# Three 256-column products in place of a 512-column one, and new address phases for weights and operands

## The chip, the cores and the metric

The kernel runs on one core of a Trainium2 chip. A core has a matrix engine (TensorE, PE in the profile), a vector engine (VectorE, DVE), a scalar engine (ScalarE, ACT), GpSimd (POOL) and the engine that issues most DMAs (SyncE, SP). The metric is the device time of one execution in microseconds. The kernel before takes 966.16 us, the median of three runs (963.55 to 966.61 us).

All work sits in two on-chip memories of 128 partitions: SBUF, which holds tiles, and PSUM, which holds matmul results in banks of 512 float32 per partition. TensorE reads two SBUF operands for each product: a stationary one (here a 128x128 block of weights, loaded by its own LDWEIGHTS instruction) and a moving one, whose columns are streamed through the array (MATMUL).

## The reference

Two layers of a bidirectional encoder trunk work on a sequence of 256 positions with model width 2048, all in float32. Each layer is, in short:

```python
hn = rmsnorm(h, norm_g[i])
u = hn @ w_in[i]                                    # 2048 x 5632
a_val, a_glu, a_z, q, k, v, b_z = split(u)
ya = swish(layernorm(conv31(a_val * sigmoid(a_glu)))) * silu(a_z)
yb = window_attention(q, k, v, bias, sink[i]) * silu(b_z)
h = h + concat([ya, yb]) @ w_out[i]                 # 2048 x 2048
e = rmsnorm(p[i] @ w_pe[i], pe_g[i])                # 256 x 2048
h = h + e * sigmoid(h @ w_pg[i])                    # 2048 x 2048
```

A last RMSNorm closes the trunk. Nearly all arithmetic is in the three large projections.

## The kernel before, in words

**Layout.** Activations lie transposed: channels on the 128 partitions, the 256 positions along the free dimension. A tensor of 2048 channels is 16 blocks of 128x256; a `big` tile holds such a tensor, or the two images (below) of half of it, in 16384 bytes per partition. There are five slots of that size.

**Split products.** TensorE's faster 32-bit form, float32r, keeps fewer bits. So each operand is split into a high image (rounded to float32r) and a low image (the rest), and one block of a projection is the sum of three products: high weight x high operand, high weight x low operand, low weight x high operand. `mm3` (L398) issues them into one accumulation in PSUM.

**Weights.** They stream from HBM as *halves*: 128x1024 float32, eight 128x128 blocks, in the order of `HALVES`. `split` (L163) makes the two images of a half: ACT writes the high one (L169), DVE the low one (L172). The result lies in one of `NSPL = 5` weight buffers, taken in turn; `SHIFT[i]` is the number of float32 by which the images are moved inside buffer i. With `SHIFT = (0, 2, 4, 8, 16)` they start 0, 8, 16, 32 and 64 bytes into the buffer. A weight tile has 2064 float32, which are 8256 bytes or 129 times 64. The operand tiles are all 16384 bytes apart, and high and low image within a tile 8192 bytes.

**Use of a half.** `steps` (L424) takes the next half or halves, and for each of its eight blocks (four in the value projection) calls `mm3`; then `pump` lets the side work (convolution taps, attention, norms) issue some instructions. There is one such call per half. In the first tile of the gate projection two halves are used in turn, block by block (`FIRST_TILES = [(0, 1), ...]`); elsewhere one half follows the other. In the value projection (L626) the roles are changed: the operand is stationary, and the weights move.

**Narrow and wide.** `mm3` has two forms. Narrow (L405 to L407): three MATMULs of 256 columns and three LDWEIGHTS per block, 24 of each per half. Wide (L402, L403), where the PSUM tile has three dimensions: the high weight is loaded once and meets both operand images in one MATMUL of 512 columns, which puts its two results side by side into one bank; the low weight then meets the high image in a MATMUL of 256 columns. That is 16 MATMULs and 16 LDWEIGHTS per half. The wide form is used in the second half of the output projection (`o<-ya`, L782) and in nearly all of the last projection (`g<-h`, `wide` L445, called in L834, L839 and L851). Its two sums have to be added afterwards: in the output projection by two DVE adds per block (L784), in the last one by `merge` (L409), which has a copy on ACT and an add on DVE, ahead of `gate` (L800).

**Order.** PE, DVE and ACT run their instructions in the order in which the code issues them. POOL's are placed by the framework.

Of the kernel before, what the change touches and what calls it, by code (L numbers as in the profile page):

```python
# [10 lines left out]
F32 = mybir.dt.float32  # L11
F32R = mybir.dt.float32r
# [5 lines left out]
P = 128  # L18
D = 2048
S = 256  # L20
DEPTH = 2
KT = D // P
# [16 lines left out]
HALF = 1024  # L39
# [9 lines left out]

NB_FIRST = KT  # L50
NSPL = 5
SHIFT = (0, 2, 4, 8, 16)
MAN = 'DVE,PE,Activation'
LY = (2, 1)
ORD = 1
# [74 lines left out]
def trunk_kernel(ctx: ExitStack, tc: tile.TileContext, xT, pT, wst, par, gain, relb, sinkp, onehot, out):  # L130
    nc = tc.nc
# [3 lines left out]
    big = ctx.enter_context(tc.tile_pool(name="big", bufs=5))  # L135
    wraw = ctx.enter_context(tc.tile_pool(name="wraw", bufs=3))
    wspl = ctx.enter_context(tc.tile_pool(name="wspl", bufs=1))
    cst = ctx.enter_context(tc.tile_pool(name="cst", bufs=1))
    wk = ctx.enter_context(tc.tile_pool(name="wk", bufs=2))
# [2 lines left out]

    def bigt(name, dt=F32):

        return big.tile([P, 2, 8, S], dt, tag="big", name=name)

    def halves(t):
        return [t[:, 0], t[:, 1]]

    def bank(name):  # L150
        return ps.tile([P, 2, S], F32, tag="ps", name=name)
# [11 lines left out]
    def split(h):  # L163
        raw = raws[h // 2][:, h % 2, :]
        i = h % NSPL
        w = wspl.tile([P, 2 * HALF + 16], F32R, tag=f"w{i}", name=f"w{h}")
        w = w[:, SHIFT[i]:SHIFT[i] + 2 * HALF].rearrange("p (t n) -> p t n", t=2)
        hi, lo = w[:, 0], w[:, 1]
        nc.scalar.copy(hi, raw)  # L169
        spl[h] = w  # L170
        if h not in (4, 5):
            nc.vector.tensor_sub(lo, raw, hi.bitcast(F32))  # L172
# [107 lines left out]
    h = halves(bigt("x"))  # L280
# [117 lines left out]
    def mm3(o, w, x, start, stop):  # L398


        if len(o.shape) == 3:
            nc.tensor.matmul(o, w[:, 0], x, start=start, stop=False, skip_group_check=True)  # L402
            nc.tensor.matmul(o[:, 1], w[:, 1], x[:, 0], start=False, stop=stop, skip_group_check=True)  # L403
            return
        nc.tensor.matmul(o, w[:, 0], x[:, 0], start=start, stop=False, skip_group_check=True)  # L405
        nc.tensor.matmul(o, w[:, 0], x[:, 1], start=False, stop=False, skip_group_check=True)  # L406
        nc.tensor.matmul(o, w[:, 1], x[:, 0], start=False, stop=stop, skip_group_check=True)  # L407

    def merge(bs):  # L409

        t = wk.tile([P, 2, S], F32, name="hl", tag="ptt")[:, 0:len(bs), :]
        for x, b in enumerate(bs):
            nc.scalar.copy(t[:, x, :], b[:, 1, :])
            nc.vector.tensor_add(t[:, x, :], b[:, 0, :], t[:, x, :])
        return t

    class Cursor:
        h = 0

    def step(o, X, start, stop):  # L420

        steps([o], X, [start], stop)
# [15 lines left out]
    def pair(X, name):  # L438
        b = bank(name)
        for x in range(2):  # L440
            step(b[:, x, :], X, x == 0, False)
            step(b[:, x, :], X, False, True)
        return b

    def wide(X, name):  # L445

        b = bank(name)
        step(b, X, True, False)
        step(b, X, False, True)
        return b  # L450

    def hilo(hi, lo, src):

        nc.scalar.copy(hi, src)
# [3 lines left out]
    for l in range(DEPTH):  # L458
# [4 lines left out]
        hg = []  # L463
        rbs, subs = [], []

        def operand(k, l=l, h=h, hg=hg):

            i, kk = k // 8, k % 8
            if kk == 0:
                hg.append(bigt(f"hg{l}_{i}", F32R))  # L470
            rb = rbs[0]
            s = wk.tile([P, 2, S], F32, name="hn", tag="u", bufs=3)
            for x in range(2):
                nc.vector.scalar_tensor_tensor(s[:, x, :], h[i][:, kk + x, :], gcol(l, k + x), rb,
                                               ALU.mult, ALU.mult)
            hi, lo = (x[:, kk:kk + 2, :] for x in halves(hg[i]))
            nc.scalar.copy(hi, s)
            return lambda: nc.vector.tensor_sub(lo, s, hi.bitcast(F32))
# [8 lines left out]
        for q in range(4):  # L487
            n = Cursor.h
            Cursor.h += 1
            if l:  # L490
                w = get(n).rearrange("p t (j k c) -> p t j k c", j=4, k=2)
            else:
                raw = raws[n // 2][:, n % 2, :].rearrange("p (j k c) -> p j k c", j=4, k=2)
            for jj in range(0, 4, 2):
                j = 4 * q + jj
                b = bank("e")
                for x in range(2):
                    for k in range(2):
                        if l:
                            mm3(b[:, x, :], w[:, :, jj + x, k, :], pp[:, :, k, :], x == 0 and k == 0, k == 1)  # L500
                        else:
                            nc.tensor.matmul(b[:, x, :], raw[:, jj + x, k, :], pf[:, k, :], start=x == 0 and k == 0,
                                             stop=k == 1, skip_group_check=True)
# [89 lines left out]
        for ts in FIRST_TILES:  # L593
            bs = [bank(f"ag{l}_{t}") for t in ts]
# [14 lines left out]
        b = pair(hg, f"k{l}")  # L609
# [9 lines left out]
        for q in range(4):  # L619
            n = Cursor.h  # L620
            Cursor.h += 1
            w = get(n).rearrange("p t (k c) -> p t k c", k=4)
            for kk in range(4):
                k = 4 * q + kk
# [65 lines left out]
        for i in range(0, 8, 2):  # L690

            b = pair(hg, f"zb{l}_{i}")
            nc.scalar.activation(zb[:, i:i + 2, :], b, AF.Silu)
            b = pair(hg, f"q{l}_{i}")

            qq = wk.tile([P, 2, 2, S], F32R, name="qq", tag="qq")
            for hh in range(2):
                r, o = rows_of[hh], rows_of[1 - hh]
# [7 lines left out]
        for t in range(0, NCT, 2):  # L706
            b = pair(hg, f"za{l}_{t}")
            if t == NCT - 2:
                finish(l)

                for k in (0, 4):
                    nc.gpsimd.dma_start(a[:, k:k + 4, :], hsrc[:, k:k + 4, :])
                yb = bigt(f"yb{l}", F32R)
                nc.scalar.copy(yb[:, 0, 0:2, :], zb[:, 0:2, :])
            nc.scalar.activation(za[:, t:t + 2, :], b, AF.Silu)

        ya = bigt(f"ya{l}", F32R)

        def lnorm(l=l, acc=acc, za=za, ya=ya, ysum=ysum, done=done):

# [42 lines left out]
        Y = [ya, yb]  # L763
        for k in (0, 4):
            nc.gpsimd.dma_start(zb[:, k:k + 4, :], hsrc[:, 8 + k:12 + k, :])
        h1 = []
# [8 lines left out]
        for j in range(0, KT, 2):  # L775
            d = az[:, j // 8, j % 8:j % 8 + 2, :]
            if j % 8 == 0:
                h1.append(bigt(f"h1{l}_{j // 8}", F32R))
            hi, lo = (x[:, j % 8:j % 8 + 2, :] for x in halves(h1[-1]))
            for x in range(2):  # L780
                b = bank(f"o{l}_{j + x}")
                step(b, Y, True, True)  # L782
                for y in range(2):
                    nc.vector.tensor_add(d[:, x, :], b[:, y, :], d[:, x, :])  # L784
            nc.scalar.copy(hi, d)
            sub = lambda d=d, hi=hi, lo=lo: nc.vector.tensor_sub(lo, d, hi.bitcast(F32))
            if j < KT - 2:
                later(sub)
            else:
                sub()  # L790
# [3 lines left out]
        last = l == DEPTH - 1  # L794
# [36 lines left out]
        hparts = []  # L831
        for j in range(0, KT - 2, 2):
            if j:
                bs = [wide(h1, f"g{l}_{j + x}") for x in range(2)]  # L834
            else:
                bs = [bank(f"g{l}_{x}") for x in range(2)]
                for n in range(2):
                    for b in bs:
                        step(b, h1, n == 0, n == 1)  # L839
            gate(j, merge(bs))  # L840
            if j == 4 and not last:
                pp = wk.tile([P, 2, 2, S], F32R, name="pp", tag="qq")
                hilo(pp[:, 0], pp[:, 1], pf)
        for j in range(KT - 2, KT):
            if last and j == KT - 1:
                b = bank(f"g{l}_{j}")[:, 0:1, :]
                step(b[:, 0, :], h1, True, False)
                step(b[:, 0, :], h1, False, True)
                gate(j, b)
            else:  # L850
                gate(j, merge([wide(h1, f"g{l}_{j}")]))  # L851
        drain()
        h = e

# [92 lines left out]
```

## Time and profile before

| | |
|---|---|
| median of three runs | 966.16 us |
| profiled execution | 963.42 us |
| its span, first to last instruction | 961.7 us |
| granted TensorE clock, mean | 0.997 |
| busy: PE, PEld, DVE, ACT, POOL | 948.5, 897.8, 792.2, 558.6, 83.6 us |

The profile was taken of one execution, which lies near the fastest of the three runs. "PE" stands for MATMUL, "PEld" for LDWEIGHTS. In groups and time lines, `g<-h,w` reads: writes tile g, reads tiles h and w; the shapes after it are those of the operands, in partitions x elements, and a MATMUL's second number is its columns. The duration of a MATMUL row (0.28 us for 256 columns) contains its passage through the array; products overlap, and the rate at which PE works is seen in the distance between the starts of two rows, not in their durations.

### The profile page before, as it was taken

What the parts mean: (1) busy time and instruction counts of PE and PEld (TensorE: products, weight loads), DVE (VectorE), ACT (ScalarE), POOL (GpSimd) and SP (SyncE); (2) the same over time, 40 slices, a digit from 0 to 9 for tenths busy, and PEclk for the clock granted to TensorE, in tenths of its full rate; (3) what the DMA queues carried; (4) which work ended last, traced back from release to release, by engine and by line L of the source; (5) the groups of instructions that cost most, each with busy time, mean ns of one, the idle gap of its engine ahead of it and who ended that gap; (6) DMA issues with size and microseconds to landing.
All of it is one profiled execution on the core that took longest, in us unless ns stands there. A gap on an engine that the chain in (4) does not pass through costs nothing.

```text
span 961.7 us, 17740 instructions
## 1 busy us (share of the span) xinstructions
PE 948.5 (99%) x7216; PEld 897.8 (93%) x7216; DVE 792.2 (82%) x1369; ACT 558.6 (58%) x861; POOL 83.6 (9%) x79
## 2 busy tenths in 40 slices
PE   8999999999999999999999999999999999999996
PEld 7999999999999998888899999999999999888885
DVE  3899989998787687887789998998887878677763
ACT  4655455777875553555566444568778545446552
POOL 0022101010000000011103200000100000000111
PEclk9999999999999999999999999999999999999998
DMA  7674546555446464546546455466454555545532
GB/s 292 224 247 175 188 164 238 197 184 188 164 160 242 153 217 165 210 175 230 204 180 220 172 198 201 176 213 206 151 172 169 190 190 193 194 168 183 178 129 88
DMA packets 29005, 182.45 MB, mean 190 GB/s; under 512 B 3595, under 2 KB 4156, under 8 KB 9084
## 3 DMA queue, kind: packets, MB, share of 16 engines
q1 hardware_dynamic: 24284, 165.70, 49.1%
q0 software_dynamic: 3344, 12.88, 4.2%
q10 hardware_dynamic: 1296, 2.75, 0.8%
q8 instruction: 56, 0.92, 0.4%
q14 instruction: 25, 0.20, 0.1%
HBM read 177.09 MB, written 4.23 MB: 189 GB/s over the span
## 4 chain that ended last, share of the span: by engine, by line
PE 94%; DVE 3%; ACT 1%; DMA 1%; issue 0%; POOL 0%; ACTq 0%; DVEq 0%
PE g L402 12%; PE o L402 6%; PE g L403 6%; PE ag L405 6%; PE ag L407 6%; PE ag L406 6%; PE za L405 3%; PE zb L405 3%; PE q L405 3%; PE o L403 3%; PE za L407 3%; PE za L406 3%; PE zb L406 3%; PE q L407 3%; PE zb L407 3%; PE q L406 3%
## 5 line engine op out<-in xcount | busy, mean ns | idle before, releaser
L172 DVE TENSOR_TENSOR w<-raw,w 128x1024 fp32r<-128x1024 f32 x306 | 373.7, 1231 | 96.0 <-ACT w L169 93.4
L169 ACT CAST w<-raw 128x1024 fp32r<-128x1024 f32 x308 | 314.1, 1048 | 142.2 <-PE ag L407 43.0
L580 DVE SCALAR_TENSOR_TENSOR cz<-az,pars,cz 128x241 f32<-128x241 f32 (+11 forms) x480 | 216.8, 501 | 1.0
L402 PE MATMUL g<-h,w 128*128 128x512 f32 x496 | 174.4, 396 | 0.0
L407 PE MATMUL ag<-hg,w 128*128 128x256 f32 x512 | 142.9, 279 | 0.5 <-DVE w L172 0.5
L405 PE MATMUL ag<-hg,w 128*128 128x256 f32 x512 | 143.3, 280 | 0.0
L406 PE MATMUL ag<-hg,w 128*128 128x256 f32 x512 | 142.7, 279 | 0.0
L403 PE MATMUL g<-h,w 128*128 128x256 f32 x496 | 139.0, 280 | 0.0
L402 PEld LDWEIGHTS g<-h,w 128*128 128x128 f32 x496 | 93.1, 188 | 22.6
L407 PEld LDWEIGHTS ag<-hg,w 128*128 128x128 f32 x512 | 96.2, 188 | 0.9 <-DVE w L172 0.9
L405 PEld LDWEIGHTS ag<-hg,w 128*128 128x128 f32 x512 | 96.2, 188 | 0.9 <-ACT w L169 0.8
L406 PEld LDWEIGHTS ag<-hg,w 128*128 128x128 f32 x512 | 96.3, 188 | 0.1
L403 PEld LDWEIGHTS g<-h,w 128*128 128x128 f32 x496 | 93.3, 188 | 0.0
L402 PE MATMUL o<-ya,w 128*128 128x512 f32 x256 | 90.1, 396 | 0.0
L405 PE MATMUL za<-hg,w 128*128 128x256 f32 x256 | 72.9, 285 | 0.0
L405 PE MATMUL q<-hg,w 128*128 128x256 f32 x256 | 72.4, 283 | 0.0
L405 PE MATMUL zb<-hg,w 128*128 128x256 f32 x256 | 72.2, 282 | 0.0
L405 PE MATMUL o<-yb,w 128*128 128x256 f32 x256 | 72.1, 282 | 0.0
L403 PE MATMUL o<-ya,w 128*128 128x256 f32 x256 | 71.7, 280 | 0.0
L407 PE MATMUL za<-hg,w 128*128 128x256 f32 x256 | 71.5, 279 | 0.0
L406 PE MATMUL za<-hg,w 128*128 128x256 f32 x256 | 71.5, 279 | 0.0
L406 PE MATMUL o<-yb,w 128*128 128x256 f32 x256 | 71.5, 279 | 0.0
(224 smaller groups left out, 2076.4 us busy)
## 6 DMA issues: line engine op xcount, KB each, us to landing
raw<-in_wst SPq DMA_DIRECT2D x153, 1024.0 KB, 4.9
bias<-fscr POOLq DMA_DIRECT2D x16, 384.0 KB, 3.8
raw<-in_wst SPq DMA_DIRECT2D x4, 512.0 KB, 8.0
az<-in_xT POOLq DMA_DIRECT2D x4, 512.0 KB, 6.1
hscr<-e POOLq DMA_DIRECT2D x2, 1024.0 KB, 5.1
az<-hscr POOLq DMA_DIRECT2D x4, 512.0 KB, 6.1
x<-in_xT SPq DMA_DIRECT2D x3, 512.0 KB, 8.3
out_t<-og ACTq DMA_DIRECT2D x4, 256.0 KB, 3.2
```

What stands on the lines that cost most here:

```text
L169: nc.scalar.copy(hi, raw)
L172: nc.vector.tensor_sub(lo, raw, hi.bitcast(F32))
L402: nc.tensor.matmul(o, w[:, 0], x, start=start, stop=False, skip_group_check=True)
L403: nc.tensor.matmul(o[:, 1], w[:, 1], x[:, 0], start=False, stop=stop, skip_group_check=True)
L405: nc.tensor.matmul(o, w[:, 0], x[:, 0], start=start, stop=False, skip_group_check=True)
L406: nc.tensor.matmul(o, w[:, 0], x[:, 1], start=False, stop=False, skip_group_check=True)
L407: nc.tensor.matmul(o, w[:, 1], x[:, 0], start=False, stop=stop, skip_group_check=True)
L580: nc.vector.scalar_tensor_tensor(acc[:, t, lo_:hi_], a[:, t, lo_ + s:hi_ + s], w(k), acc[:, t, lo_:hi_], ALU.mult, ALU.add)
```

## The change: narrow products everywhere, other phases

1. `mm3` loses its wide form, and `wide` and `merge` go. The 94 wide halves (32 of the output projection, 62 of the last one) are issued as narrow ones: 24 MATMULs of 256 columns and 24 LDWEIGHTS per half, where there were 16 and 16. Pairs of output blocks share one PSUM bank; one DVE add of 512 columns per pair takes the place of four of 256 in the output projection, and `gate` reads the bank itself.
2. The weight buffers' shifts become 16, 24, 32, 48 and 56 float32 (64, 96, 128, 192 and 224 bytes). A weight tile now has 2112 float32, 8448 bytes or 132 times 64.
3. Operand tiles get phases of their own (`bigx`). A slot of `big` has 24 float32 more, so 16480 bytes, 32 more than a multiple of 64. The tile of the first eight blocks starts at its slot's start, that of the second eight 16 bytes on (`XSHIFT`), and the low image of each lies 8192 + 32 bytes behind the high one (`XLOW`).

```diff
-SHIFT = (0, 2, 4, 8, 16)
+SHIFT = (16, 24, 32, 48, 56)
+XSHIFT = (0, 4)
+XLOW = 8
...
     def bigt(name, dt=F32):
 
-        return big.tile([P, 2, 8, S], dt, tag="big", name=name)
+        return big.tile([P, 16 * S + 24], dt, tag="big", name=name)[:, 0:16 * S].rearrange(
+            "p (t k s) -> p t k s", t=2, k=8)
+
+    def bigx(name, i):
+
+        n = 8 * S + XLOW
+        t = big.tile([P, 16 * S + 24], F32R, tag="big", name=name)[:, XSHIFT[i]:XSHIFT[i] + 2 * n]
+        return t.rearrange("p (t n) -> p t n", t=2)[:, :, 0:8 * S].rearrange("p t (k s) -> p t k s", k=8)
...
-        w = wspl.tile([P, 2 * HALF + 16], F32R, tag=f"w{i}", name=f"w{h}")
+        w = wspl.tile([P, 2 * HALF + 64], F32R, tag=f"w{i}", name=f"w{h}")
...
     def mm3(o, w, x, start, stop):
 
 
-        if len(o.shape) == 3:
-            nc.tensor.matmul(o, w[:, 0], x, start=start, stop=False, skip_group_check=True)
-            nc.tensor.matmul(o[:, 1], w[:, 1], x[:, 0], start=False, stop=stop, skip_group_check=True)
-            return
         nc.tensor.matmul(o, w[:, 0], x[:, 0], start=start, stop=False, skip_group_check=True)
         nc.tensor.matmul(o, w[:, 0], x[:, 1], start=False, stop=False, skip_group_check=True)
         nc.tensor.matmul(o, w[:, 1], x[:, 0], start=False, stop=stop, skip_group_check=True)
...
-                hg.append(bigt(f"hg{l}_{i}", F32R))
+                hg.append(bigx(f"hg{l}_{i}", i))
...
-                yb = bigt(f"yb{l}", F32R)
+                yb = bigx(f"yb{l}", 1)
...
-        ya = bigt(f"ya{l}", F32R)
+        ya = bigx(f"ya{l}", 0)
...
-                h1.append(bigt(f"h1{l}_{j // 8}", F32R))
+                h1.append(bigx(f"h1{l}_{j // 8}", j // 8))
             hi, lo = (x[:, j % 8:j % 8 + 2, :] for x in halves(h1[-1]))
+            b = bank(f"o{l}_{j}")
             for x in range(2):
-                b = bank(f"o{l}_{j + x}")
-                step(b, Y, True, True)
-                for y in range(2):
-                    nc.vector.tensor_add(d[:, x, :], b[:, y, :], d[:, x, :])
+                step(b[:, x, :], Y, x == 0, True)
+            nc.vector.tensor_add(d, b, d)
...
             if j:
-                bs = [wide(h1, f"g{l}_{j + x}") for x in range(2)]
+                b = pair(h1, f"g{l}_{j}")
             else:
-                bs = [bank(f"g{l}_{x}") for x in range(2)]
+                b = bank(f"g{l}_{j}")
                 for n in range(2):
-                    for b in bs:
-                        step(b, h1, n == 0, n == 1)
-            gate(j, merge(bs))
+                    for x in range(2):
+                        step(b[:, x, :], h1, n == 0 and x == 0, n == 1)
+            gate(j, b)
...
         for j in range(KT - 2, KT):
-            if last and j == KT - 1:
-                b = bank(f"g{l}_{j}")[:, 0:1, :]
-                step(b[:, 0, :], h1, True, False)
-                step(b[:, 0, :], h1, False, True)
-                gate(j, b)
-            else:
-                gate(j, merge([wide(h1, f"g{l}_{j}")]))
+            b = bank(f"g{l}_{j}")[:, 0:1, :]
+            for n in range(2):
+                step(b[:, 0, :], h1, n == 0, n == 1)
+            gate(j, b)
```

More of the change, by code (lines that the diff above doesn't have):

```diff
@@ L407, in mm3 @@
         nc.tensor.matmul(o, w[:, 1], x[:, 0], start=False, stop=stop, skip_group_check=True)
[L409 to L415, printed above, removed]
     class Cursor:
@@ L443, in pair @@
         return b
[L445 to L450, printed above, removed]
     def hilo(hi, lo, src):
```

## The prediction, made before the changed kernel was run

> **What bounds the kernel now.** I read the page of the profile first: how busy each engine is, the granted clock, and the chain that ended last.
>
> ```profile
> PE 948.5 (99%) x7216; PEld 897.8 (93%) x7216; DVE 792.2 (82%) x1369; ACT 558.6 (58%) x861; POOL 83.6 (9%) x79
> ...
> PEclk9999999999999999999999999999999999999998
> ...
> PE 94%; DVE 3%; ACT 1%; DMA 1%; issue 0%; POOL 0%; ACTq 0%; DVEq 0%
> ```
>
> PE works nearly all the time at full clock, and the chain runs along it for 94% of the span. Then the list of PE's waits, all of those after the start-up:
>
> ```profile
> PE ag L407 <- DVE w L172: 0.5, 1, 0.5
> PE rfc L355 <- ACT sq L815: 0.4, 1, 0.4
> PE rv0b L369 <- POOL rv0col L362: 0.2, 1, 0.2
> ```
>
> That is 1.1 us. So the time is set by the distance between PE's products, and the groups and the time lines have to say what that is. The groups count them:
>
> ```profile
> L169 ACT CAST w<-raw 128x1024 fp32r<-128x1024 f32 x308 | 314.1, 1048 | 142.2 <-PE ag L407 43.0 <-PE za L407 20.0 <-PE q L407 19.8
> L402 PE MATMUL g<-h,w 128*128 128x512 f32 x496 | 174.4, 396 | 0.0
> L402 PE MATMUL o<-ya,w 128*128 128x512 f32 x256 | 90.1, 396 | 0.0
> ```
>
> 308 halves are split. 496 + 256 = 752 wide MATMULs, eight per half, make 94 wide halves; the other 214 are narrow, 214 x 24 = 5136 products. ACT waits for PE to free weight buffers: PE is what the others wait for.
>
> **What a wide half costs.** Its stages begin and end in these time lines (start in us, duration):
>
> ```profile
> 345.75 0.39 PE L402 MATMUL o<-ya,w 128*128 128x512 f32 x1
> 480.74 0.28 PE L405 MATMUL e<-pp,w 128*128 128x256 f32 x1
> 812.74 0.39 PE L402 MATMUL o<-ya,w 128*128 128x512 f32 x1
> 942.10 0.28 PE L405 MATMUL g<-h,w 128*128 128x256 f32 x1
> ```
>
> In layer 0, 134.99 us hold 16 + 32 = 48 wide halves, in layer 1, 129.36 us hold 46: 2.812 us per half both times. Over the 24 products that the change makes of it, this is 117.2 ns each.
>
> **What a narrow half costs.** The first products of halves 29, 31, 32, 33 and 34 (counted in the order of use; half h lies in buffer h mod 5):
>
> ```profile
> 96.63 0.28 PE L405 MATMUL ag<-hg,w 128*128 128x256 f32 x1
> 102.08 0.28 PE L405 MATMUL ag<-hg,w 128*128 128x256 f32 x1
> 104.91 0.28 PE L405 MATMUL ag<-hg,w 128*128 128x256 f32 x1
> 107.71 0.28 PE L405 MATMUL ag<-hg,w 128*128 128x256 f32 x1
> 110.56 0.28 PE L405 MATMUL ag<-hg,w 128*128 128x256 f32 x1
> ```
>
> Buffers 4 and 0 together: 5.45 us for 48 products, 113.5 ns each. Buffer 1: 2.83/24 = 117.9. Buffer 2: 116.7. Buffer 3: 118.8. Same instruction, same operand tiles; only the weights' address differs. All tile sizes before are multiples of 64 bytes, so the distance from operand to weights, modulo 64, is the shift: 0 in buffers 4 and 0 (64 and 0 bytes), then 8, 16 and 32. So distance 0 is fast, the others cost 3 to 5 ns more. (Buffers 4 and 0 are alike modulo far more than 64, so a longer period isn't excluded.) Longer stretches, with 24, 32 and 10 halves:
>
> ```profile
> 54.83 0.28 PE L405 MATMUL ag<-hg,w 128*128 128x256 f32 x1
> 121.64 0.50 PE L355 MATMUL re0c<-ones,fold 128*128 128x1 f32 x4
> 504.72 0.28 PE L405 MATMUL ag<-hg,w 128*128 128x256 f32 x1
> 594.61 0.28 PE L405 MATMUL v<-w,hg 128*128 128x256 f32 x1
> 605.88 0.28 PE L405 MATMUL zb<-hg,w 128*128 128x256 f32 x1
> 634.14 0.28 PE L648 MATMUL sc<-keys0h,qq 128*128 128x256 f32 x1
> ```
>
> 66.81/576 = 116.0, 89.89/768 = 117.0, 28.26/240 = 117.8 ns. In the third, the same buffers at the same distances no longer reach 113.5: the fast pace is a rhythm that can be missed. For narrow products as a whole I take the first two together, 156.7/1344 = 116.6 ns.
>
> **The change part by part.** *Width.* 94 halves become narrow: 94 x 24 = 2256 products at the new pace r, in place of 117.2 ns. So 752 MATMULs and 752 LDWEIGHTS more cost nothing by themselves: 512 columns already took about two narrow distances. The term is 2256 x (r - 117.2).
>
> *Phases.* All other products change pace too: 5136 x (r - 116.6). One ns of r is worth 7.4 us; this is the whole case. After the change a weight tile is 132 x 64 bytes and an operand slot 32 more than a multiple of 64; with the shifts, weights stand at 0 or 32 modulo 64. The first operand tile's images stand at 0 and 32, the second's at 16 and 48. So in each half on the first tile one image is at distance 0 and the other at 32, on the second tile at 16 and 48; a quarter of the work falls to each. Distance 48 is in no narrow row with the present roles. Its nearest rows are in the value projection, where the weights move (halves 41, 42, and the start of 43):
>
> ```profile
> 131.03 0.28 PE L405 MATMUL v<-w,hg 128*128 128x256 f32 x1
> 133.91 0.28 PE L405 MATMUL v<-w,hg 128*128 128x256 f32 x1
> 136.77 0.28 PE L405 MATMUL v<-w,hg 128*128 128x256 f32 x1
> ```
>
> Half 41 (buffer 1) takes 120.0 ns per product, half 42 (buffer 2, with roles changed at -16, that is 48) 119.2. Bounds for distance 48: 113.5 to 120.0. I take the middle of 116.7 (distance 16) and 119.2, which is 118. The plain mean of the four is then (113.5 + 116.7 + 118.8 + 118)/4, about 116.7.
>
> But the plain mean supposes that a product keeps its pace beside one of another distance. Rows on that are in the first tile of the gate projection, where two halves alternate block by block (halves 8/9, 160/161, 162/163 and 166/167; 504.72 stands above):
>
> ```profile
> 36.77 0.28 PE L405 MATMUL ag<-hg,w 128*128 128x256 f32 x1
> 42.37 0.28 PE L405 MATMUL ag<-hg,w 128*128 128x256 f32 x1
> ...
> 493.37 0.28 PE L405 MATMUL ag<-hg,w 128*128 128x256 f32 x1
> 499.05 0.28 PE L405 MATMUL ag<-hg,w 128*128 128x256 f32 x1
> 510.17 0.28 PE L405 MATMUL ag<-hg,w 128*128 128x256 f32 x1
> 515.82 0.28 PE L405 MATMUL ag<-hg,w 128*128 128x256 f32 x1
> ```
>
> Buffers 3 and 4 alternating, distances 32 and 0: 5.60/48 = 116.7, where the mean of their own paces is 116.2. Buffers 0 and 1 (0 and 8): 118.3 against 115.7. Buffers 2 and 3: 118.1 against 117.7. Buffers 1 and 2: 117.7 against 117.3. Only 4 and 0, both at distance 0, keep 113.5 (504.72 to 510.17). So mixing costs 0.4 to 2.6 ns. The dear case, 0 with 8, doesn't occur after the change; but these rows change distance once in three products, and the change does so twice in every three (high, low, high image). I add 0.7 ns, a little over the 0.5 of 0 with 32: **r = 117.4**. Bounds: 115.6 (no cost of mixing, 48 as fast as 0) and 120.0.
>
> *The adds.* These go or shrink:
>
> ```profile
> L413 ACT COPY hl<-g 128x256 f32<-128x256 f32 x31 | 11.5, 370 | 19.1 <-PE g L403 19.1
> L414 DVE TENSOR_TENSOR hl<-g,hl 128x256 f32<-128x256 f32 x31 | 12.2, 418 | 5.6 <-ACT hl L413 5.6
> L784 DVE TENSOR_TENSOR az<-o,az 128x256 f32<-128x256 f32 x64 | 27.0, 422 | 2.0 <-PE o L403 0.9
> L772 DVE TENSOR_TENSOR az<-o,az 128x512 f32<-128x512 f32 x16 | 11.0, 686 | 1.1 <-PE o L407 1.1
> ...
> 345.75:480.74 134.99, 134.99 (x771) 117.50 (x770) 104.08 (x148) 67.62 (x89) 8.39 (x7) 1.00 0.57 202
> ```
>
> ACT loses 11.5 us, DVE 12.2 + 27.0 - 16 x 0.686 = 28 us. The last row is the stage 345.75 to 480.74 (busy PE, PEld, DVE, ACT): PE fills all 134.99 us while DVE has 31 us to spare, so this is off the path: 0. The only place where a merge could stand on it is the end of layer 0, 0.370 + 0.418 = 0.8 us, and there the next layer's four halves of `w_pe` cover it; in layer 1 the last block has no merge already. Bounds: -0.8 to 0. Operand tiles, weight images and DMAs at other offsets I put at 0 too: no row shows DVE's or ACT's speed hanging on the weights' phase, and DVE and ACT wait for PE, not PE for them. PSUM needs fewer banks.
>
> *Sum.* 5136 x 0.8 ns + 2256 x 0.2 ns = 4.1 + 0.5 = **+4.6 us**, which makes 968.0 of the profiled execution's 963.4 us. The median of the runs, 966.16, is 2.7 us above that execution; the same step is carried over: **970.8 us**, 0.5% slower.
>
> **Rivals.** *Plain mean.* Each product keeps the pace of its own distance, r = 116.7: +0.5 - 1.1 = -0.6 us, 965.5. For it: the first long stretch, 116.0, is the mean of its buffers' own paces. Against it: the alternating halves.
>
> *Faster: the fast rhythm spreads.* Mechanism: distance 0 is fast because the two streams fall into step, and 48 does as well; no operand is left at an odd 8 bytes; no cost of mixing. r = 115.6: -5.1 - 3.6 = -8.7 us, 957.5. It decides from r = 116.4 down, where the two terms come to -2.9 us. Against it: 119.2 in half 42, and that wide halves in buffers 4 and 0 aren't faster than the rest.
>
> *Every product as in half 41.* r = 120.0: 17.5 + 6.3 = +23.8 us, 990. For it: a moving operand not at a multiple of 64, as there. Against it: that offset was 8 bytes, inside a 16-byte unit, and here all are multiples of 16.
>
> *The phases do nothing.* New narrow products run at today's mean: 2256 x (116.6 - 117.2) = -1.4 us, 964.8. The five halves above speak against it. The Trainium skill, page "SBUF — State Buffer", section "Who interferes with whom", would have it so: TensorE has two independent read ports, one for the moving operand and one for LDWEIGHTS, and never waits on anyone. The trace disagrees: with nothing but the weights' address changed, 113.5 becomes 118.8 ns.
>
> **How the numbers follow.** Forecast 0.50; plain mean and phases without effect together 0.28; the rhythm spreads 0.17; as half 41 0.05. A measurement of this kernel tells about 0.3% (2.9 us) from no change. The forecast's lower edge reaches into that, so faster 0.18, same 0.32, slower 0.50. The range goes from the fast rival, 957, to a mixing cost of 2 ns, r = 118.7, +14.2 us: 981 rounded up. The forecast's own range, r = 117.0 to 118.2, is 968 to 977.
>
> **What would show it.** PE's waits stay near 1 us, and no row of L402 with 512 columns is left. 24 products per half in the last projection start 117 to 118 ns apart; halves on the first operand tile and on the second differ, and no stretch of 48 holds 113.5. Wrong it is if such stretches are common, if starts come 116.5 ns apart or 119 and more, or if PE waits for weights.

## The result, and the profile after

The changed kernel takes 972.81 us, the median of three runs (972.66 to 975.30), against 966.16 us before. The comparison of the two gives a ratio of 1.0092, with a 95% interval of 1.0073 to 1.0110: the change makes the kernel 0.9% slower. The profiled execution after takes 972.81 us with a span of 971.0 us; before it was 963.42 us and 961.7 us. So between the two profiles, from which all stages below are read, there are 9.4 us. The medians of before and after are only 6.7 us apart, since the three runs of before lie 0.1 to 3.2 us above its profiled execution.

The page of the changed kernel, in the order in which the prediction read it (busy time of the engines, granted clock, shares of the chain that ended last):

```profile
PE 958.1 (99%) x7968; PEld 941.5 (97%) x7968; DVE 769.8 (79%) x1290; ACT 550.3 (57%) x830; POOL 83.6 (9%) x79
...
PEclk9999999999999999999999999999999999999998
...
PE 94%; DVE 3%; ACT 1%; DMA 1%; issue 0%; POOL 0%; ACTq 0%; DVEq 0%
```

There are 752 MATMULs and 752 LDWEIGHTS more, as worked out, and PE is still the chain, at the same clock. PE is busy for 9.6 us more, and that is the whole loss. From the changed kernel's list of PE's waits (total, times, longest, in us), the longest of the start-up and the longest after it, both as long before:

```profile
PE rh0c L364 <- DVE fold L388: 1.7, 1, 1.7
...
PE ag L412 <- DVE w L181: 0.5, 1, 0.5
```

No wait has been added: the engine starts its products farther apart. Two rows of its groups (busy us, mean ns of one, idle time before it and its cause):

```profile
L410 PE MATMUL g<-h,w 128*128 128x256 f32 x512 | 143.7, 281 | 0.0
L773 DVE TENSOR_TENSOR az<-o,az 128x512 f32<-128x512 f32 x16 | 11.1, 691 | 6.5 <-PE o L412 6.5
```

The last projection has no row with 512 columns left, and DVE waits for PE at its new, wider adds. Where the time went is in the time lines of the changed kernel (start and duration in us) at the same places as before: the beginning and the end of layer 0's former wide stage, then the beginning of layer 1's and the 46th half after it.

```profile
349.07 0.28 PE L410 MATMUL o<-ya,w 128*128 128x256 f32 x1
484.98 0.28 PE L410 MATMUL e<-pp,w 128*128 128x256 f32 x1
820.80 0.28 PE L410 MATMUL o<-ya,w 128*128 128x256 f32 x1
951.45 0.28 PE L410 MATMUL g<-h,w 128*128 128x256 f32 x1
```

In layer 0, 135.91 us hold 48 halves of 24 products: 118.0 ns each, where a wide half came to 117.2. In layer 1, 130.65 us hold 46 halves: 118.3 ns. The stages that were narrow already lose more. From the first gate product (24.08 us before, 23.94 after) to the first row there were 321.7 us before and are 325.1 now; from the second row to the third there were 332.0 and are 335.8. So +3.5 and +3.8 us stand there, and +0.9 and +1.3 in the two stages that were wide: 9.5 us in all.

The same halves as in the prediction, 29 to 34, here the starts of halves 29, 32, 33 and 34:

```profile
97.14 0.28 PE L410 MATMUL ag<-hg,w 128*128 128x256 f32 x1
105.67 0.28 PE L410 MATMUL ag<-hg,w 128*128 128x256 f32 x1
108.52 0.28 PE L410 MATMUL ag<-hg,w 128*128 128x256 f32 x1
111.36 0.28 PE L410 MATMUL ag<-hg,w 128*128 128x256 f32 x1
```

Halves 29 to 31 take 8.53 us, 118.5 ns per product; half 32 takes 118.8, half 33 118.3. The spread between buffers, 113.5 to 118.8 ns before, is nearly gone, and it closed at the slow end. Over all products of the changed kernel whose distance to the next isn't widened by a wait or by other work (at most 126 ns), the mean is 118.05 ns. That is the r of the prediction, which had 117.4.

### The profile page after: what moved, and what is told of

Read it like the earlier page. It is cut to its first block, busy times and chain, and to the rows that moved or that the text cites. A ratio compares the mean times of both kernels' runs of the same rounds, so it can differ in the third digit from the quotient of the medians.

```text
span 971.0 us, 19136 instructions
## 1 busy us (share of the span) xinstructions
PE 958.1 (99%) x7968; PEld 941.5 (97%) x7968; DVE 769.8 (79%) x1290; ACT 550.3 (57%) x830; POOL 83.6 (9%) x79
## 4 chain that ended last, share of the span: by engine, by line
PE 94%; DVE 3%; ACT 1%; DMA 1%; issue 0%; POOL 0%; ACTq 0%; DVEq 0%
PE g L411 6%; PE g L410 6%; PE g L412 6%; PE ag L411 6%; PE ag L410 6%; PE ag L412 6%; PE o L411 6%; PE o L410 6%; PE o L412 6%; PE za L410 3%; PE zb L410 3%; PE q L410 3%; PE q L411 3%; PE za L411 3%; PE zb L411 3%; PE zb L412 3%
## 5 line engine op out<-in xcount | busy, mean ns | idle before, releaser
L181 DVE TENSOR_TENSOR w<-raw,w 128x1024 fp32r<-128x1024 f32 x306 | 374.1, 1231 | 117.2 <-ACT w L178 116.7
L411 PE MATMUL g<-h,w 128*128 128x256 f32 x512 | 143.8, 281 | 0.0
L410 PE MATMUL g<-h,w 128*128 128x256 f32 x512 | 143.7, 281 | 0.0
L412 PE MATMUL g<-h,w 128*128 128x256 f32 x512 | 143.5, 280 | 0.0
L410 PEld LDWEIGHTS g<-h,w 128*128 128x128 f32 x512 | 96.7, 189 | 0.0
L411 PEld LDWEIGHTS g<-h,w 128*128 128x128 f32 x512 | 96.5, 188 | 0.0
L412 PEld LDWEIGHTS g<-h,w 128*128 128x128 f32 x512 | 96.4, 188 | 0.0
L410 PE MATMUL za<-hg,w 128*128 128x256 f32 x256 | 73.2, 286 | 0.0
L410 PE MATMUL q<-hg,w 128*128 128x256 f32 x256 | 72.7, 284 | 0.0
L410 PE MATMUL o<-yb,w 128*128 128x256 f32 x256 | 72.5, 283 | 0.0
L411 PE MATMUL za<-hg,w 128*128 128x256 f32 x256 | 72.0, 281 | 0.0
L411 PE MATMUL q<-hg,w 128*128 128x256 f32 x256 | 72.0, 281 | 0.0
```

## The experiments

Unless a diff says otherwise, each is an edit of the changed kernel. Paces are start to start, per product of 256 columns; "the mean of the clean ones" is the mean over distances of at most 126 ns, as just now. "Distance" is, as in the prediction, the address of the weights less that of the moving operand.

### Width alone, phases alone

The first kernel is narrow everywhere and has the tile sizes and shifts of before:

```diff
-SHIFT = (16, 24, 32, 48, 56)
-XSHIFT = (0, 4)
-XLOW = 8
+SHIFT = (0, 2, 4, 8, 16)
+XSHIFT = (0, 0)
+XLOW = 0
...
-        t = big.tile([P, 16 * S + 24], F32R, tag="big", name=name)[:, XSHIFT[i]:XSHIFT[i] + 2 * n]
+        t = big.tile([P, 16 * S + 0], F32R, tag="big", name=name)[:, XSHIFT[i]:XSHIFT[i] + 2 * n]
-        w = wspl.tile([P, 2 * HALF + 64], F32R, tag=f"w{i}", name=f"w{h}")
+        w = wspl.tile([P, 2 * HALF + 16], F32R, tag=f"w{i}", name=f"w{h}")
```

> The width alone: all products narrow, weights and operands where they were before. Theory (the phases cost, the width does not): the 94 halves that were wide run at the present narrow pace, 116.0 to 117.0 ns per product, so 2256 x (116.5 - 117.2) = -1.6 us, about 964.6 us, not told from no change. Rival (the width costs: 752 more LDWEIGHTS and MATMULs): most of the 6.65 us is here, about 972 us, and the products of the last projection start 119 ns apart or more.

Measured: 961.96 us against 964.37 us of before on the same chip, ratio 0.9971 (0.9958 to 0.9984). Four starts of this kernel, at the places used above:

```profile
347.16 0.28 PE L410 MATMUL o<-ya,w 128*128 128x256 f32 x1
480.79 0.29 PE L410 MATMUL e<-pp,w 128*128 128x256 f32 x1
812.64 0.28 PE L410 MATMUL o<-ya,w 128*128 128x256 f32 x1
940.71 0.28 PE L410 MATMUL g<-h,w 128*128 128x256 f32 x1
```

The 48 halves of layer 0 take 133.63 us, 116.0 ns per product, where the wide form took 134.99 us; the 46 of layer 1 take 128.07 us, 116.0 ns. So with the old phases the narrow form gains 1.4 and 1.3 us, and the two stages that were narrow before stay at 321.7 and 331.9 us. 752 more instructions of each kind cost nothing, as the prediction put it.

The second has the new tile sizes and shifts and keeps the two forms of `mm3`, with `wide`, `merge` and what calls them as before:

```diff
     def mm3(o, w, x, start, stop):
+        if len(o.shape) == 3:
+            nc.tensor.matmul(o, w[:, 0], x, start=start, stop=False, skip_group_check=True)
+            nc.tensor.matmul(o[:, 1], w[:, 1], x[:, 0], start=False, stop=stop, skip_group_check=True)
+            return
...
```

> The phases alone: the wide products stay, weights and operands lie as in the changed kernel. Theory: the 5136 narrow products go from 116.6 to 118.0 ns, +7.2 us, and the wide ones stay near 2.81 us per half, so about 973 us. Rival (the width costs): near 966 us.

Measured: 970.91 us against 964.37, ratio 1.0067 (1.0052 to 1.0082). The stages that are narrow in it take 325.2 and 335.8 us, as in the changed kernel; the wide ones take 134.88 us for the 48 halves of layer 0 and 129.40 us for the 46 of layer 1, where it was 134.99 and 129.36 before. Its group of wide products in the last projection:

```profile
L411 PE MATMUL g<-h,w 128*128 128x512 f32 x496 | 174.2, 396 | 0.0
```

Before, the same row had 396 ns as well. So the loss comes from the phases, and over a whole stage only narrow products feel them. (Single wide halves differ a little from buffer to buffer: before, those of layer 0 took 2.793 us in buffer 1 and 2.826 us in buffers 0 and 3.) The new phases cost 6.5 us on 5136 narrow products, 10.9 us on 7392 (972.81 less 961.96); in its own stages the width is a gain of 1.4 and 1.3 us with the old phases and a loss of 0.9 and 1.3 us against before with the new ones.

### Which distances are fast

The prediction took distances modulo 64 and called 0 the fast one. Two kernels test this. In the first every weight image stands at distance 0 from every operand image, modulo 256 too; in the second at distance 64.

Both put the operand tiles back to 16384 bytes apart with no shift of their own; in the first a weight tile has 8192 bytes.

```diff
-SHIFT = (16, 24, 32, 48, 56)
-XSHIFT = (0, 4)
-XLOW = 8
+SHIFT = (0, 0, 0, 0, 0)
+XSHIFT = (0, 0)
+XLOW = 0
...
-        w = wspl.tile([P, 2 * HALF + 64], F32R, tag=f"w{i}", name=f"w{h}")
+        w = wspl.tile([P, 2 * HALF + 0], F32R, tag=f"w{i}", name=f"w{h}")
```

> The changed kernel with no shift at all: every weight buffer and every operand image begins at the same address modulo 8192 bytes (modulo 64 too). Theory (distance 0 modulo 64 is fast, and stays fast where nothing else is mixed in): all products at 113.5 ns, 7392 x (113.5 - 118.05) = -33.6 us against the changed kernel, about 940 us. Rival (the period is longer than 64 bytes and only a distance of 64 is fast): about 118 ns, 972 us or more. Second rival (the fast rhythm comes from the change between buffers): slower than before, about 970 us.

Measured: 987.94 us against 964.37, ratio 1.0239 (1.0224 to 1.0255). Starts of halves 136 and 156 in this kernel:

```profile
434.99 0.28 PE L410 MATMUL g<-h,w 128*128 128x256 f32 x1
492.59 0.28 PE L410 MATMUL e<-pp,w 128*128 128x256 f32 x1
```

57.60 us for 480 products: 120.0 ns, and each half took 2.880 us. The distance that the prediction took for the fast one is slower than every half with the usual roles in its rows (113.5 to 118.8 ns), and it has the "120.0" of its dearest rival.

For distance 64, with the changed kernel's weight tiles:

```diff
-SHIFT = (16, 24, 32, 48, 56)
+SHIFT = (16, 16, 16, 16, 16)
+XSHIFT = (0, 0)
+XLOW = 0
```

> As the kernel without shifts, but all weight buffers 64 bytes on (all at distance 64 modulo 256 from the operands, as buffers 4 and 0 before). Theory (period of 64 bytes): the same time as without shifts, about 940 us. Rival (only the distance of 64 is fast, period 128 or more): this one 940 us and the one without shifts 972 us.

Measured: 954.54 us, ratio 0.9889 (0.9866 to 0.9912). Starts of halves 100, 122, 262 and 310:

```profile
321.99 0.28 PE L410 MATMUL o<-yb,w 128*128 128x256 f32 x1
384.18 0.28 PE L410 MATMUL o<-ya,w 128*128 128x256 f32 x1
804.35 0.28 PE L410 MATMUL o<-yb,w 128*128 128x256 f32 x1
934.91 0.28 PE L410 MATMUL g<-h,w 128*128 128x256 f32 x1
```

Between the first two, 62.19/528 = 117.8 ns; between the last two, 130.56/1152 = 113.3 ns. The instructions and the distance are the same in both stretches. So 64 bytes is not the period (0 and 64 would be alike), distance 64 can run at 113.3 ns, and it has a second, slower rhythm, which it kept in layer 0 from half 99 to half 155 once it had fallen into it.

### A table of distances

The changed kernel with one shift per half in place of one per buffer: in the output projection's second half and the last projection, six halves each at distances 0, 16, 32 and so on, up to 112 in layer 0 and from 128 to 240 in layer 1. Four stretches of six halves near the start of each layer have other distances, and the rest is at 64. Here and in the kernels below, but for the one on mixing, the operand tiles lie 16384 bytes apart again.

```diff
+SHIFT = (0, 0, 0, 0, 0)
+XSHIFT = (0, 0)
+XLOW = 0
+def shift_of(h):
+    l, r = divmod(h, NHALF)
+    if r >= 108:
+        return 4 * ((r - 108) // 6 + 8 * l)
+    if 14 <= r < 38:
+        return ((2, 18, 34, 50), (16, 48, 32, 24))[l][(r - 14) // 6]
+    return 16
...
-        w = w[:, SHIFT[i]:SHIFT[i] + 2 * HALF].rearrange("p (t n) -> p t n", t=2)
+        w = w[:, shift_of(h):shift_of(h) + 2 * HALF].rearrange("p (t n) -> p t n", t=2)
```

> A scan of distances in one kernel. All operand images at one phase; the weights' distance to them (modulo 256 bytes) is 64 except here: the last 48 halves of layer 0 take 0, 16, ... 112 bytes, six halves each, those of layer 1 128 to 240, and four stretches of six halves at the start of each layer take 8, 72, 136, 200 and 64, 192, 128, 96. Theory (a distance sets the pace, with a period over 64 bytes): the paces repeat what is known, 0 at 120.0, 8 near 118, 32 near 118.8, 64 at 113.3 or 117.8, 208 at 116.7, and each stretch has one pace of its own; the mean of the sixteen is near 117.0. Rival (only the rhythm taken over from the half before decides): stretches of the same distance differ, and after the stretch at 64 the following ones keep 113.3.

Measured: 963.91 us in one run, before 964.08; the time itself says nothing here, the time lines do. First products at distances 0 to 112 and the end of the last, then at 128 to 240 and, four halves on, the last but one half:

```profile
344.38 0.28 PE L421 MATMUL o<-ya,w 128*128 128x256 f32 x1
361.66 0.28 PE L421 MATMUL o<-ya,w 128*128 128x256 f32 x1
378.70 0.28 PE L421 MATMUL o<-ya,w 128*128 128x256 f32 x1
395.74 0.28 PE L421 MATMUL g<-h,w 128*128 128x256 f32 x1
412.70 0.28 PE L421 MATMUL g<-h,w 128*128 128x256 f32 x1
429.02 0.28 PE L421 MATMUL g<-h,w 128*128 128x256 f32 x1
446.13 0.28 PE L421 MATMUL g<-h,w 128*128 128x256 f32 x1
463.22 0.28 PE L421 MATMUL g<-h,w 128*128 128x256 f32 x1
480.50 0.29 PE L421 MATMUL e<-pp,w 128*128 128x256 f32 x1
...
811.75 0.28 PE L421 MATMUL o<-ya,w 128*128 128x256 f32 x1
828.84 0.28 PE L421 MATMUL o<-ya,w 128*128 128x256 f32 x1
846.11 0.28 PE L421 MATMUL o<-ya,w 128*128 128x256 f32 x1
863.39 0.28 PE L421 MATMUL g<-h,w 128*128 128x256 f32 x1
880.39 0.28 PE L421 MATMUL g<-h,w 128*128 128x256 f32 x1
897.35 0.28 PE L421 MATMUL g<-h,w 128*128 128x256 f32 x1
914.15 0.28 PE L421 MATMUL g<-h,w 128*128 128x256 f32 x1
930.95 0.28 PE L421 MATMUL g<-h,w 128*128 128x256 f32 x1
942.47 0.28 PE L421 MATMUL g<-h,w 128*128 128x256 f32 x1
```

Each difference is 144 products (the last one 96), so 361.66 - 344.38 = 17.28 us is 120.0 ns:

```
distance   0    16    32    48    64    80    96   112   128   144   160   176   192   208   224   240
ns      120.0 118.3 118.3 117.8 113.3 118.8 118.7 120.0 118.7 119.9 120.0 118.1 117.8 116.7 116.7 120.0
```

The mean of the sixteen is 118.3 ns. Neither 64 nor 128 is a period. In this kernel the weight buffers lie 256 bytes apart modulo 512, and from half to half the pace doesn't alternate, so 256 is one. With that the rows of before fall into place. The addresses that follow from its tile sizes and the order of first use (buffer 4, then 0 to 3) give distances of 64 in buffers 4 and 0, 136 in buffer 1, 208 in buffer 2 and 32 in buffer 3; other halves of this kernel at 136 ran at 118.0, and the table has 116.7 at 208 and 118.3 at 32. The prediction's rows had 113.5, 117.9, 116.7 and 118.8.

But each value stands for one stretch, and a distance can have more than one pace. Distance 96 ran at 117.4 ns in halves 190 to 192 of the same kernel, where the table has 118.7; the starts of halves 190 and 193:

```profile
578.66 0.28 PE L421 MATMUL ag<-hg,w 128*128 128x256 f32 x1
587.11 0.28 PE L421 MATMUL k<-hg,w 128*128 128x256 f32 x1
```

Half 156 took 2.88 us before and 2.74 us in the kernel with the width alone, at the same addresses.

The same with steps of 8 bytes between, and some of 4; all other halves stand at 8:

```diff
...
+    if r >= 108:
+        return (6, 10, 14, 22, 26, 30, 38, 42, 46, 54, 58, 62, 1, 3, 15, 17)[(r - 108) // 6 + 8 * l]
+    return 2
...
```

> A second scan, of distances that are no multiple of 16 bytes. All weights at distance 8, except the last 48 halves of each layer, six halves each: 24, 40, 56, 88, 104, 120, 152, 168 bytes in layer 0, 184, 216, 232, 248, 4, 12, 60, 68 in layer 1. Theory (the pace is set by the distance modulo 256, finer than in 16 bytes): 4, 12 and 60, 68 are not all alike; most lie between 116 and 120 ns, and next to none at 113.3. Rival (whole 16-byte units count): 4 and 12 have the pace of 0 (120.0), 60 that of 48 (117.8), 68 that of 64.

Measured: 965.41 us in one run, before 963.61. Worked out from the starts in the two scans' traces, here as the median half of each stretch (8, 72, 136 and 200 from the first scan):

```
distance   8    24    40    56    72    88   104   120   136   152   168   184   200   216   232   248
ns      115.6 121.7 119.2 117.8 118.3 113.3 120.0 119.4 118.0 117.8 120.0 117.8 116.7 120.0 117.7 117.6
distance   4    12    60    68
ns      118.3 116.7 119.6 118.3
```

No step of 16, 8 or 4 bytes can be left out: 16, 24 and 32 have 118.3, 121.7 and 118.3 ns, and 4, 8 and 12 have 118.3, 115.6 and 116.7. The pace follows the low bits of the address down to single words.

In the scans all large operand tiles stand at one phase, so that the weights' own address would explain them as well as the distance does. The halves of `w_pe` in layer 1 tell the two apart, since their operand `pp` lies at another phase. By the addresses in the built programs, the weights at distance 64 from the large operand tiles are at 160 from `pp`: in the kernel with all at 64, halves 156 and 159 took 2.881 and 2.880 us, the 120.0 ns that the table has at 160. In the changed kernel half 159 alone meets its operand at 64 with all its products, and it is fast, 2.73 us or 113.8 ns (starts of halves 159 and 160):

```profile
494.80 0.28 PE L410 MATMUL e<-pp,w 128*128 128x256 f32 x1
497.53 0.28 PE L410 MATMUL ag<-hg,w 128*128 128x256 f32 x1
```

### Does mixing cost anything

In the changed kernel each half meets two distances: the high operand image at d (both weight images, 16 products), the low one at d - 32 (8 products). The prediction added 0.7 ns for that. This kernel has the high image at 64 and the low one at 32 in every half of the large projections (in the value projection, with the roles changed, at -64 and -32); an operand slot has 64 float32 more in place of 24, and a weight tile 8192 bytes:

```diff
+SHIFT = (0, 0, 0, 0, 0)
+XSHIFT = (48, 48)
 XLOW = 8
...
```

> Mixing alone: all weights at distance 64 from every high operand image, as in the kernel with all at 64, but each low image 32 bytes on, so that the distance is 64 for two products in three and 32 for the third. Theory (mixing in every block breaks the fast rhythm): 117.5 to 118.5 ns, about 970 us, slower than the kernel before and some 16 us slower than with all at 64. Rival (each product keeps the pace of its own distance): (113.3 + 118.8 + 113.3)/3 = 115.1 ns where the fast rhythm holds, 950 to 955 us.

Measured: 978.99 us against 964.08, ratio 1.0150 (1.0133 to 1.0167). Halves 264 and 310:

```profile
826.82 0.28 PE L410 MATMUL o<-ya,w 128*128 128x256 f32 x1
958.07 0.28 PE L410 MATMUL g<-h,w 128*128 128x256 f32 x1
```

131.25/1104 = 118.9 ns. Two products at 113.3 and one at 118.3 would make 115.0 each; with 64 at its slower rhythm, 118.0. So a single product at 32 in every three takes away the fast rhythm of the other two, and costs 0.9 ns more than the slow one. Mixing is a real cost where a fast distance is in the mix. In the changed kernel that is a small part. All 16 distances occur in it (301 to 547 each of some 7100 clean products outside the value projection, by the addresses in the built program), and the table gives, product by product, 118.3 ns as the mean of its halves without a cost of mixing. Measured is 118.05. Half 32, at 64 and 32, ran 3.8 ns slower than its mean of 115.0; but half 139, at 144 and 112, ran at 115.9 where the table has 119.9. For a single half the table is no guide there (the correlation of worked-out and measured times over 300 halves is -0.13); over the kernel the two sides cancel.

### What sends a stream into the slow rhythm, and out of it

Here one buffer of five is at 32 and the others at 64:

```diff
+SHIFT = (16, 16, 16, 8, 16)
+XSHIFT = (0, 0)
+XLOW = 0
...
```

> Can the fast rhythm be held? All operand images at one phase, four weight buffers at distance 64 and buffer 3 at 32. With all five at 64 the pace was 113.3 or 117.8 ns, and the slow one lasted until an interruption; in the kernel before, the buffers behind buffer 3 were nearly always fast. Theory (a half at another distance shifts the two streams, and they fall into the fast rhythm again): (4 x 113.4 + 118.5)/5 = 114.4 ns, 7392 x (114.4 - 118.05) = -27 us against the changed kernel, about 946 us. Rival (chance decides at every re-entry): between 115.3 and 117 ns, 952 to 965 us, no better than with all at 64.

Measured: 959.90 us against 964.08, ratio 0.9936 (0.9909 to 0.9963). Times of single halves, worked out from the starts in its trace (us; every fifth is the half at 32):

```
halves  99-109  2.723 2.720 2.720 2.723 | 2.837 | 2.720 2.720 2.720 2.723 | 2.837 | 2.720
halves 289-299  2.829 2.826 2.827 2.828 | 2.837 | 2.828 2.827 2.827 2.828 | 2.837 | 2.828
```

A half at 32 leaves the rhythm of the others as it was: fast stays fast, and slow stays slow in 17 of the 18 halves at 32 that follow a slow one, outside the value projection, with no interruption near. The exception is half 168: the half before it took 2.827 us, the two behind it 2.736 and 2.720. So that it sets the stream right as a rule, or throws it out, falls. What decides the rhythm stays open here; the six runs of this kernel go from 953.98 to 962.31 us. In before, the two fast buffers, 4 and 0, come after buffer 2 at 208 and buffer 3 at 32. This kernel has such a pair every ten halves, and 64 in the other eight:

```diff
...
+def shift_of(h):
+    return {8: 52, 9: 8}.get(h % 10, 16)
...
-        w = w[:, SHIFT[i]:SHIFT[i] + 2 * HALF].rearrange("p (t n) -> p t n", t=2)
+        w = w[:, shift_of(h):shift_of(h) + 2 * HALF].rearrange("p (t n) -> p t n", t=2)
```

> As the kernel with all weights at distance 64, but of every ten halves one stands at 208 and the next at 32, as in buffers 2 and 3 of the kernel before, behind which the buffers at 64 were nearly always fast. Theory (the two streams keep a rhythm, and this pair of halves leaves the one that is fast at 64): (8 x 2720 + 2800 + 2840)/10 = 2740 ns per half where nothing else interrupts, 114.7 ns over all, about 950 us, below the kernel with all at 64 (954.5). Rival (the rhythm behind such a pair is chance too): 115.5 to 117 ns, 956 to 966 us.

Measured: 952.11 us against 963.61, ratio 0.9881 (0.9865 to 0.9898). Starts of halves 108, 110 and 118; 108 and 109 are the pair at 208 and 32:

```profile
344.18 0.28 PE L416 MATMUL o<-ya,w 128*128 128x256 f32 x1
349.82 0.28 PE L416 MATMUL o<-ya,w 128*128 128x256 f32 x1
371.61 0.28 PE L416 MATMUL o<-ya,w 128*128 128x256 f32 x1
```

The halves ahead of the pair, 101 to 107, took 2.826 to 2.827 us each. The eight after it take 21.79/192 = 113.5 ns, the first 2.741 us and the others 2.720 to 2.724. In the kernel with all at 64 the halves from 99 to 155 are slow throughout. This is the one pair outside the value projection that meets a slow stream without an interruption. Where an interruption falls into the pair itself, it needn't help: behind 98 and 99, and behind 188 and 189, the halves up to the next pair took 2.825 to 2.829 us. Nor does it take just this pair: in the first scan the stream was fast at 64 at once behind six halves at 48 (half 132, 2.721 us). Two halves in ten pay 116.7 and 118.2 ns for it, so that the gain over all at 64 is 2.4 us by the medians, with intervals that overlap.

### Versions that stay at one distance

Two more distances of the table are fast, 8 and 88. The kernels are those of distance 64 with another shift.

```diff
+SHIFT = (2, 2, 2, 2, 2)
```

> All weights at distance 8 bytes from all operand images (modulo 256). In the scan six halves in a row took 2773 ns there, 115.6 per product. Theory (a distance that has only one rhythm): 115.6 ns all over, 7392 x (115.6 - 118.05) = -18 us against the changed kernel, about 954 us or a little below. Rival (the 115.6 was taken over from the fast halves before it): 117 to 118 ns, 965 to 972 us.

Measured: 957.27 us against 963.61, ratio 0.9938 (0.9920 to 0.9956). It has one rhythm only: halves 264 to 310 take 127.58 us, 115.6 ns per product, and after each interruption of the stream it is back at once. In the value projection, where the weights are the moving operand, its halves take 2.880 us, 120.0 ns; the distance there is -8, that is 248, for which the table has 117.6, so with the roles changed it isn't a sure guide.

```diff
+SHIFT = (22, 22, 22, 22, 22)
```

> All weights at distance 88 bytes from all operand images (modulo 256). In the second scan six halves in a row took 2720 ns there, the fast pace, coming from a half of 2826. Theory (distance 88 has the fast rhythm and is drawn into it from any other): 113.4 ns nearly everywhere, 7392 x (113.4 - 118.05) = -34 us against the changed kernel, some 940 us. Rival (88 has a second, slow rhythm as 64 has): 115 to 116 ns, 952 to 958 us.

Measured: 947.47 us (947.27 to 949.11) against 964.80, ratio 0.9827 (0.9811 to 0.9844). This beats before and after. Halves 264 and 310:

```profile
801.08 0.28 PE L410 MATMUL o<-ya,w 128*128 128x256 f32 x1
926.20 0.28 PE L410 MATMUL g<-h,w 128*128 128x256 f32 x1
```

125.12/1104 = 113.3 ns. This distance has two rhythms too, but the slow one is 2.800 us per half, 116.7 ns (halves 165 to 184, for instance), where it is 117.8 at distance 64; and from half 99 to 155 and from 255 to 311 it ran fast throughout. The mean of the clean products is 114.43 ns, 3.6 below the changed kernel's; 7392 x 3.6 ns is 26.6 us, and the two profiled spans, 945.5 and 971.0, are 25.5 apart.

## Why the prediction was right or wrong

**What bounds the kernel.** Right. PE's waits and its clock stayed as they were, and the product's distance times 7392 accounts for the change: 5136 x (118.05 - 116.6) + 2256 x (118.05 - 117.2) = 7.4 + 1.9 = 9.3 of 9.4 us.

**The adds.** Right at zero. In this row of the changed kernel (layer 0's former wide stage: busy PE, PEld, DVE, ACT, POOL, then clock and DMA) DVE has 42 us to spare, 31 before, and PE has no gap:

```profile
349.07:484.98 135.91, 135.91 (x1154) 135.91 (x1153) 94.00 (x110) 64.10 (x74) 8.37 (x7) 1.00 0.57 201
```

**Width.** Right that it costs nothing by itself; with the old phases it was worth -2.4 us, where 2256 x (116.6 - 117.2) had made -1.4.

**Phases.** The direction was right and the time, 970.8 against 972.81, close; the working under it was not. The step that failed is the distance "modulo 64". Buffers 4 and 0 were fast because both stood at 64 modulo 256, and not because they stood at 0 modulo 64. The four distances of the changed kernel are sixteen, of which one is fast and five have 119.9 or 120.0: their mean is 118.3 and not 116.7. The prediction saw the gap ("a longer period isn't excluded") and then counted a quarter of the products at the fast pace. In the rows of before the two periods can't be told apart, since only four distances occur in them. Its other reading, that the fast pace is a rhythm that can be missed, was right, as the kernel at 64 shows.

**The cost of mixing.** The 0.7 ns stood in for part of what the wrong period had left out. As a term of the whole it should have been -0.25 (118.05 less 118.3). As a mechanism it exists and is larger than assumed: 3.9 ns against the mean of the paces in the kernel at 64 and 32. The term r was 0.65 ns short, which is 4.8 us over 7392 products: 968.0 was worked out for the profiled execution, and 972.8 was measured. The total came closer than that because the step of 2.7 us from the profiled execution to the median was carried over; after the change the profiled execution is the median itself. So it is in part luck that 970.8 lies so near to 972.81: against a plain mean of 118.3, the wrong period took away 7392 x 1.6 ns = 11.8 us, and the cost of mixing (0.7 where it should have been -0.25) and the step to the median gave back 7.0 and 2.7.

**The price of distance 48.** 118 was taken from bounds of 113.5 and 120.0; 48 runs at 117.8. The row with 119.2, half 42, stands at 48 too, with the roles changed.

**The rivals.** *The plain mean*: as an average it holds, and with all sixteen distances in it, it makes 118.3 where 118.05 was measured. Its mechanism, that each product keeps the pace of its own distance, does not: half by half the table is no guide, and at 64 and 32 the products ran 3.9 ns above their mean. *The fast rhythm spreads* fell: but for half 159, all of which is at 64, no half of the changed kernel ran below 2.773 us, 115.5 ns. *Every product as in half 41* describes the kernel at distance 0, 987.94 us, and not this change. *The phases do nothing* fell in the kernel with the phases alone, 0.5 to 0.8% slower. By the Trainium skill, page "SBUF — State Buffer", section "Who interferes with whom", TensorE's two read ports are independent; the kernels at 0 and at 88, with the same instructions in the same order, take 987.94 and 947.47 us, so independent ports as the page has them do not make the addresses indifferent.

**What would show it.** The halves on the two operand tiles do differ, 118.2 ns on the first and 117.9 on the second, but the other way round than the prediction's paces would have it: (113.5 + 118.8)/2 and (116.7 + 118)/2 make 116.2 and 117.4. Starts in the last projection came 118 ns apart, within what was named.

## What to carry to other kernels

Where TensorE is the bound, and products of 256 columns each load their own weights, try all weight buffers at one distance from the moving operand, modulo 256 bytes, choose it by a scan within one kernel, and then time the whole kernel at it, since a distance can have a second pace: here 88 bytes gives 947 us and 0 gives 988 us, with the same instructions in the same order. Spreading the phases evenly gave about the mean of good and bad here, and one image at 32 in each block took the fast pace from the products at 64. A period that is inferred from a few addresses is a guess until an address that breaks it has been run.

## What the hardware showed that was not expected

The distance between narrow products hangs on the address of the weights less that of the operand, modulo 256 bytes and down to 4 bytes: 113.3 ns at 64 and 88, 120.0 at 0, 121.7 at 24. The stages of wide halves, with products of 512 columns in them, don't show it: they took 134.88 and 129.40 us with the new phases and 134.99 and 129.36 with the old.

At distances 64 and 88 the same instructions run at one of two paces (113.3 or 117.8, 113.3 or 116.7 ns), each often kept for tens of halves until something interrupts the stream. Other distances have more than one pace as well: 96 ran at 118.7 and 117.4, and half 156, at the same addresses, at 2.88 and 2.74 us. At 8 only one was seen, 115.6. A pair of halves at 208 and 32 brought the fast pace at 64 back in the one case where it met a slow stream without an interruption; a single half at 32 did so once in 18.

The Trainium skill, page "TensorE: Matmul & The Clock Gate", section "Back-to-back issue gap", gives N/2.4 + 2.5 ns for isolated products at full clock, an estimate of 109.2 ns for 256 columns. The fastest pace of any half here is 113.3, and the range of 113 to 122 isn't in it.

What makes the distance matter is open. A clash between the reading of weights and of the moving operand would fit a dependence on their difference, but no run here separates it from other causes; nor is it settled what decides between the two paces, or why mixed halves such as 139 run faster than either of their distances alone.
